# Eight split slots and four load buffers instead of six and six, weight parts made five blocks ahead within a stage, other queue orders behind the norms, and gate groups that begin with one

## The chip, the core and the metric

The kernel runs on one core of a Trainium2 chip. A core has five engines with instruction streams of their own: TensorE (PE: matmuls, with the weight load as PEld), VectorE (DVE), ScalarE (ACT), GpSimd (POOL) and SyncE (SP), which here issues the DMAs. They wait for each other by semaphores. On each engine instructions run in a fixed order, so one that waits holds up everything behind it. The metric is device time in microseconds, the median of several runs.

## The reference

Two layers work on 256 tokens of 1024 features. Layer 0 mixes by latent attention (MLA): a low-rank input projection, RMS norms, up-projections to queries, keys and values of 8 heads, rotary embedding, attention by chunks of 64, an output projection. Layer 1 mixes by sparse attention (DSA): an indexer scores keys, the best 64 keys per query are kept, then attention over those. After each mixer comes

```
x = layernorm(alpha * x + m);  f = peer(x);  x = layernorm(alpha * x + f)
```

and `peer` is a retrieval among 16384 experts:

```
q = (xt @ w_q);  s1, s2 = q against sub_keys          # 16 rows of 128 scores a token
v1, i1 = top_k(s1, 16);  v2, i2 = top_k(s2, 16)
best, pos = top_k(v1 + v2, 16);  gate = softmax(best)
a = x . w_down[expert];  y = sum(gelu(a) * gate * w_up[expert])
```

The kernel does not gather expert rows: it multiplies all tokens by all of `w_down`, places the gates of the chosen experts in a table of 256 x 16384, multiplies, and multiplies all of that by `w_up`.

## The kernel before

**Weights as a stream of blocks.** Every weight matrix is cut into blocks of 128 x 1024 f32 (512 KB), taken in one fixed order by `Stream` (`ws`). A block is loaded by SP into a buffer `raw` (pool `raws`, 6 buffers), and then split into two f16 parts: `hi` on ACT (line 89) and `lo = raw * unit - hi` on DVE (line 98). A slot of the pool `rings` (6 of them, for `hi` and for `lo`) is free again when PE has done the block. PE multiplies in three passes (hi by hi, hi by low, low by hi), which replace one f32 product. `get()` hands out the next block and has the splits emitted up to `AHEAD` = 3 blocks further (`_split`), and the loads up to `DMA_AHEAD` = 5 blocks beyond that (`_load`). A load waits until the split of the block six loads earlier has read its buffer.

**Pooled splits.** Where `ws.share` is n, every n-th block takes another way (`_pooled`): ACT scales `raw` in place (line 164) and casts it to `hi` (line 166), POOL subtracts (line 168), and ACT reads `lo` once more for a check sum (`_add`, line 177). Line 164 needs the loaded buffer but no slot of the ring.

**Stages.** In order: MLA projections and attention with `out_proj`; PEER 0: `queries` and `scores`, 128 `down` blocks in pairs, 128 `up` blocks; DSA; PEER 1 likewise. `finish` closes each stage: the last four blocks are multiplied first for token half 0, then for half 1, while half 0 goes through its `Norm` (`sums`, `square`, `centre`, `scale`, `result`); then `Turned` turns it by PE and splits it (`high` on ACT, `low` on DVE). Meanwhile PE takes the first blocks of the next stage (`open` makes `hi`, `close` makes `lo`) in units `do(t, part, k)`: token half t, one of the three products ("hh", "lh": low x by hi weights, "hl": hi x by low weights), block k. The queue helper of `finish` forces the written order on each engine.

**Choosing.** In `peer` the choice (`choose`) runs on DVE beside the first 58 `down` blocks. `spend(PACE)` is called once per block and emits as much of it as fits a written-down cost; `chains["dve"]` then holds DVE to exactly the order of emission, splits included. It ends in `gates`: four transposes on PE (`gT`, line 1177) and DVE ops that yield `gate16`, `rest` and `place16`. From then on each pair of `down` blocks has `want` groups of four tokens prepared (`prepare`: `hot` on DVE, line 1240; `gate` on POOL, line 1242, and on ACT, line 1246), and the next pair places them (`place`: matmuls `G` on PE, between the pair's matmuls and the next pair's).

**Order.** Where no chain, `issue_after` or queue helper says so, the scheduler of the language orders each engine's instructions by its own cost model, with the program's order as priority; so the order on ACT is partly decided there. In DSA, DVE is chained from the first key heads on, ACT only from the middle of `attention`.

Of the kernel before, what the change touches and what calls it, by code (L numbers as in the profile page):

```python
# [15 lines left out]
ALU = mybir.AluOpType  # L16
# [4 lines left out]
D = 1024  # L21
# [25 lines left out]
WARM = 9  # L47
EARLY = 11264
GSCALE = 2.0 ** 14
RING = 6  # L50
LAG = 4
DSA_POOL = 3
MAGIC = 12582912.0
# [1 line left out]
W_UNIT = 2.0 ** 17  # L55
# [4 lines left out]
UP_UNIT = 2.0 ** 14  # L60
# [9 lines left out]
class Split:  # L70


    def __init__(self, nc, short, cols):
        self.nc, self.short, self.cols = nc, short, cols
        self.n = {"both": 0, "most": 0}
        self.at = {"both": (0, BOTH), "most": (BOTH, BOTH + MOSTLY)}
# [24 lines left out]
class Stream:  # L101


    AHEAD = 3
    DMA_AHEAD = 5

    def __init__(self, nc, raw, rings, dtype, split, spare):
        self.nc, self.raw, self.rings, self.dtype, self.split, self.spare = nc, raw, rings, dtype, split, spare
        self.dve = self.act = lambda emit: emit()
        self.blocks, self.ready, self.kind = [], [], []  # L110
        self.n_loaded = self.n_split = self.n_taken = 0
        self.tiles = []
        self.early = {}
        self.share = 0
        self.late = {}

    def add(self, src, w=D, unit=W_UNIT, kind="both"):
        for i in range(src.shape[0]):
            self.blocks.append((src[i], w, unit))
            self.kind.append(kind)  # L120

    def parts(self, i):
        w = self.blocks[i][1]
        return [self.rings.tile([P, D], self.dtype, tag=k, name=f"{k}{i}")[:, :w] for k in ("hi", "lo")]
# [52 lines left out]
            self.act(lambda: self.nc.scalar.activation(self.spare[:, : lo.shape[1]], lo, AF.Copy, accum_out=total))  # L177

    def _split(self, upto, pooled):
        while self.n_split <= min(upto, len(self.blocks) - 1):  # L180
            i = self.n_split
            if pooled or self.share and (i - 1) % self.share == 0:
                self._pooled(i)
            else:
                self._high(i, self.act)
                self._low(i, self.dve)
            self._add(i - LAG)
            self.n_split += 1

    def get(self, ahead=None, pooled=False):  # L190
        i = self.n_taken
        self.n_taken += 1
        self.fill(i + (self.AHEAD if ahead is None else ahead), pooled)
        return self.ready[i]
# [10 lines left out]
    def close(self, i, queue):  # L205
        self._low(i, lambda emit: queue("dve", emit))
        self._load(i + self.DMA_AHEAD + 1)

    def fill(self, upto, pooled=False):
        self._split(upto, pooled)  # L210
        self._load(upto + self.DMA_AHEAD)

# [29 lines left out]
def tile_trunk(ctx: ExitStack, tc: tile.TileContext, ins, out: bass.AP, short, shared):  # L242
    nc = tc.nc
    half = F16 if short else F32R
    unit, ranks, total_unit = (UNIT, RANKS, SUM) if short else (1.0, 1.0, 1.0)
    def pool(name, bufs, **kw):
        return ctx.enter_context(tc.tile_pool(name=name, bufs=bufs, **kw))

    lead = pool("lead", 1)
    wide = pool("wide", 1)  # L250
    raws = pool("raws", 6 if short else 4)
    rings = pool("rings", RING if short else 4)
    const = pool("const", 1)
    dram = pool("dram", 1, space=bass.MemoryType.DRAM)
# [8 lines left out]
    def ps(name):  # L263
        return psp.tile([P, 512], F32, tag="ps", name=name)
# [7 lines left out]
    split = Split(nc, short, const.tile([P, BOTH + MOSTLY], F32, tag="sums", name="sums") if short else None)  # L272
# [27 lines left out]
    ws = Stream(nc, raws, rings, half, split, spare16)  # L300
    ws.add(ins["mla_h"][0:6])
    ws.add(ins["mla_qk"], unit=RANK_W_UNIT)
    ws.add(ins["mla_v"], unit=RANK_W_UNIT)
    ws.add(ins["mla_w_o"])
    ws.add(ins["peer_q"][0])
    ws.add(ins["down"][0], kind="most")
    ws.add(ins["up"][0], unit=UP_UNIT, kind="most")
    ws.add(ins["dsa_v"][0:FIRST])
    ws.add(ins["dsa_iq"])
    ws.add(ins["dsa_ik"], 576)  # L310
    ws.add(ins["dsa_v"][FIRST:NC])
    ws.add(ins["dsa_qk"])
    ws.add(ins["dsa_w_o"])
    ws.add(ins["peer_q"][1])
    ws.add(ins["down"][1], kind="most")
    ws.add(ins["up"][1], unit=UP_UNIT, kind="most")
# [90 lines left out]
    class Norm:  # L407
# [18 lines left out]
            self.queue("act", lambda: nc.scalar.activation(self.sq, self.r, AF.Square, bias=st[:, 2:3],  # L426
                                                           accum_out=st[:, 3:4]))

        def centre(self):
            st = self.st  # L430
            self.queue("dve", lambda: nc.vector.scalar_tensor_tensor(self.z, self.r, st[:, 2:3], self.g,
                                                                     op0=ALU.add, op1=ALU.mult))

        def scale(self):
            st = self.st
# [36 lines left out]
    def finish(y4, lhs_of, n, g, b, x, spare, lead=None):  # L472

        blks = [ws.get(ahead=0) for _ in range(STAGGER)]
        queue = queue_of()
        last = None
        norms = []  # L480
        for t in range(2):
            with ExitStack() as order:
                if last is not None:
                    order.enter_context(tc.issue_after(last.ins))
                for i, blk in enumerate(blks):
                    k = n - STAGGER + i
                    last = rows(y4, lhs_of(k), blk, k == 0, k == n - 1, (t,))
            if lead is not None:
                norms.append(Norm(queue, x[t], y4[t], g, b, spare[t], spare[2 + t], spare[4]))
        if lead is None:  # L490
            if short:
                judge()

            def close():
                queue = queue_of()
                for t in range(2):
                    norm = Norm(queue, x[t], y4[t], g, b, spare[t], spare[2 + t], spare[4], shared["st"][t])
                    norm.sums()
                    norm.square()
                    norm.centre()  # L500
                    norm.scale()
                    norm.result()
                for t in range(2):
                    for h, q in enumerate((nc.sync, nc.scalar)):
                        s = slice(h * 512, (h + 1) * 512)
                        q.dma_start(out[t * P : (t + 1) * P, s], spare[t][:, s])

            return close
        n0, n1 = norms
        n0.sums()  # L510
        n0.square()
        n0.centre()
        n0.scale()
        n0.result()
        nc.sync.dma_start(keep[0], spare[0])
        queue("pe", lambda: last)
        x0, x1 = Turned(queue, 0, spare[0]), Turned(queue, 1, spare[1])
        blk = [ws.open(queue) for _ in range(3)]
        n1.sums()
        x0.high(0, 2)  # L520
        x0.high(1, 4)
        n1.square()
        x0.low(0)
        n1.centre()
        blk.append(ws.open(queue))
        n1.scale()
        x0.low(1)
        n1.result()
        nc.sync.dma_start(keep[1], spare[1])
        unit = lead(queue)  # L530

        def do(t, part, *ks):
            for k in ks:
                unit(t, part, k, ws.ready[blk[k]])

        do(0, "hh", 0, 1, 2)
        do(0, "lh", 0, 1, 2)
        do(0, "hh", 3)
        do(0, "lh", 3)
        x1.high(0, 2)  # L540
        x1.high(1, 4)
        do(1, "hh", 0, 1, 2, 3)
        ws.close(blk[0], queue)
        ws.close(blk[1], queue)
        x1.low(0)
        do(0, "hl", 0, 1)
        do(1, "lh", 0, 1)
        do(1, "hl", 0, 1)
        ws.close(blk[2], queue)
        x1.low(1)  # L550
        do(0, "hl", 2)
        do(1, "hl", 2)
        do(1, "lh", 2)
        ws.close(blk[3], queue)
        do(0, "hl", 3)
        do(1, "hl", 3)
        do(1, "lh", 3)
# [491 lines left out]
    def peer(li):  # L1049
# [4 lines left out]
        s = [ar.take(16, NKEYS) for _ in range(2)]  # L1054
# [209 lines left out]
        groups = prepared = 0  # L1264
        ready = False
        for b0 in range(0, NKEYS, 2):
            p = ps(f"d{b0}")
            pv = p.rearrange("p (j t) -> p j t", t=T)
            chosen = ready
            for j in range(2):  # L1270
                proj(pv[:, j, :], ws.get())
                ready = ready or spend(PACE)
            if b0 == 0:
                chains["pe"] = None
            t0 = 4 * groups
            if t0 < T:
                nc.scalar.activation(A[:, b0 : b0 + 2, t0:], pv[:, :, t0:], AF.Gelu, scale=1.0 / unit)
            if t0 > 0:
                nc.scalar.activation(pv[:, :, :t0], pv[:, :, :t0], AF.Gelu, scale=1.0 / unit)
                nc.vector.tensor_tensor(A[:, b0 : b0 + 2, :t0], A[:, b0 : b0 + 2, :t0], pv[:, :, :t0], op=ALU.mult)  # L1280
            while groups < prepared:
                place(groups, b0 + 2)
                groups += 1
            if chosen:
                left = max(1, (NKEYS - 4 - b0) // 2)
                want = min(64 - groups, -(-(64 - groups) // left))
                assert want <= 2
                for _ in range(want):
                    prepare(prepared)
                    prepared += 1  # L1290
# [98 lines left out]

    mla()  # L1390
    peer(0)
    dsa()
    return peer(1)


# [89 lines left out]
```

## Time and profile before

| what | before |
|---|---|
| median of 3 runs | 1729.37 us (1728.97 to 1731.33) |
| profiled execution, its time | 1731.02 us |
| its span, first to last instruction | 1729.1 us |
| PE busy | 1702.9 us (98%) |
| DVE busy | 1346.9 us (78%) |
| ACT busy | 1096.5 us (63%) |
| POOL busy | 393.5 us (23%) |
| mean granted TensorE clock | 0.998 |

The span and the execution's own time differ by 1.9 us that lie outside the first and last instruction. Busy shares are means over stages with different limits, and ends of matmuls are modelled. So what counts is where PE sat idle, and which engine released it; the views named in the prediction give that.

### The profile page before, as it was taken

What the parts mean: (1) busy time and instruction counts of PE and PEld (TensorE: products, weight loads), DVE (VectorE), ACT (ScalarE), POOL (GpSimd) and SP (SyncE); (2) the same over time, 40 slices, a digit from 0 to 9 for tenths busy, and PEclk for the clock granted to TensorE, in tenths of its full rate; (3) what the DMA queues carried; (4) which work ended last, traced back from release to release, by engine and by line L of the source; (5) the groups of instructions that cost most, each with busy time, mean ns of one, the idle gap of its engine ahead of it and who ended that gap; (6) DMA issues with size and microseconds to landing.
All of it is one profiled execution on the core that took longest, in us unless ns stands there. A gap on an engine that the chain in (4) does not pass through costs nothing.

```text
span 1729.1 us, 33166 instructions
## 1 busy us (share of the span) xinstructions
PE 1702.9 (98%) x12497; PEld 1193.2 (69%) x12497; DVE 1346.9 (78%) x3033; ACT 1096.5 (63%) x1908; POOL 393.5 (23%) x257
## 2 busy tenths in 40 slices
PE   9999999999999999999998999999999999999998
PEld 7678888899984444444577698888999954444443
DVE  7679999989996566566687799999899966566565
ACT  7666556888875555555476756567888755555553
POOL 3011254555530000000022012444555400000000
PEclk9999999999999999999999999999999999999999
DMA  9445556655567666666564555566555576666662
GB/s 330 156 168 175 187 191 202 213 173 171 172 194 237 204 205 202 203 205 205 190 237 147 196 171 175 193 205 221 172 171 172 178 247 204 202 205 204 201 204 77
DMA packets 93483, 335.61 MB, mean 194 GB/s; under 512 B 10368, under 2 KB 11392, under 8 KB 93312
## 3 DMA queue, kind: packets, MB, share of 16 engines
q1 hardware_dynamic: 93024, 332.87, 59.4%
q8 instruction: 100, 1.64, 0.4%
q14 instruction: 71, 0.58, 0.1%
q10 hardware_dynamic: 288, 0.52, 0.1%
HBM read 329.16 MB, written 4.19 MB: 193 GB/s over the span
## 4 chain that ended last, share of the span: by engine, by line
PE 86%; DVE 7%; issue 3%; ACT 2%; DMA 1%; POOL 1%; DVEq 0%; SPq 0%; POOLq 0%; ACTq 0%
PE y L340 40%; PE d L340 33%; PE G L340 3%; DVE lo L98 2%; PE pq L340 2%; PE qw L340 1%; ACT hi L89 1%; PE v L340 1%; PE s L340 1%; PE o L340 1%; PE h L340 1%; DMA raw<-in_down 1%; PE ps L340 1%; PE q L340 1%; PE qi L340 1%
## 5 line engine op out<-in xcount | busy, mean ns | idle before, releaser
L98 DVE SCALAR_TENSOR_TENSOR lo<-raw,hi 128x1024 f16<-128x1024 f32 (+1 forms) x571 | 776.1, 1363 | 234.4 <-ACT hi L89 233.4
L89 ACT ACTIVATE hi<-raw 128x1024 f16<-128x1024 f32 (+1 forms) x570 | 594.8, 1051 | 294.3 <-PE y L340 183.3
L340 PE MATMUL d<-xh,lo 128*128 128x256 f16 x2048 | 558.3, 273 | 3.0 <-DVE lo L98 2.4
L340 PE MATMUL d<-xh,hi 128*128 128x256 f16 x2048 | 558.2, 273 | 0.0
L340 PE MATMUL d<-xl,hi 128*128 128x256 f16 x2048 | 558.2, 273 | 0.0
L340 PEld LDWEIGHTS <-hi 128*128 128x128 f16 x5016 | 488.5, 98 | 58.8 <-issue 1.8
L340 PEld LDWEIGHTS <-xh 128*128 128x128 f16 x2320 | 226.4, 98 | 270.6 <-ACT xh L89 2.4
L340 PE MATMUL y<-lo,xh 128*128 128x512 f16 x1088 | 326.3, 379 | 0.0
L340 PE MATMUL y<-hi,xh 128*128 128x512 f16 x1088 | 326.0, 379 | 0.0
L340 PE MATMUL y<-hi,xl 128*128 128x512 f16 x1088 | 325.6, 379 | 0.0
L340 PEld LDWEIGHTS <-lo 128*128 128x128 f16 x2508 | 245.4, 98 | 35.1 <-DVE lo L98 5.6
L1242 POOL TENSOR_TENSOR gate<-hot,gate 128x512 f16<-128x512 f16 x128 | 219.5, 1734 | 187.0 <-DVE hot L1240 187.0
L340 PEld LDWEIGHTS <-xl 128*128 128x128 f16 x1160 | 113.3, 98 | 138.2 <-DVE xl L98 2.5
L1246 ACT ACTIVATE gate<-hot,rest 128x128 f16<-128x128 f16 x512 | 165.9, 411 | 8.2 <-DVE hot L1240 8.2
L89 ACT ACTIVATE xh<-arena 128x512 f16<-128x512 f32 x131 | 82.0, 629 | 133.6 <-PE y L340 132.2
L98 DVE SCALAR_TENSOR_TENSOR xl<-arena,xh 128x512 f16<-128x512 f32 x134 | 91.9, 688 | 61.0 <-ACT xh L89 60.8
L168 POOL TENSOR_TENSOR lo<-raw,hi 128x1024 f16<-128x1024 f32 x26 | 58.1, 2234 | 192.2 <-ACT hi L166 150.8
L438 POOL TENSOR_TENSOR st<-st,mhalf 128x1 f32<-128x1 f32 x6 | 3.3, 556 | 414.2 <-DVE st L436 414.2
L164 ACT ACTIVATE raw<-raw 128x1024 f32<-128x1024 f32 x26 | 27.4, 1056 | 110.4 <-DMA raw<-in_down 91.0
L1164 POOL TENSOR_TENSOR arena<-arena 128x800 f32<-128x800 f16 x32 | 72.4, 2263 | 71.6 <-DVE arena L1161 63.4
L1240 DVE TENSOR_TENSOR hot<-iota,place 128x1024 f16<-128x1024 f16 x128 | 82.8, 689 | 6.4 <-PE G L340 3.9
L580 POOL TENSOR_SCALAR fit<-fit 128x2 f32<-128x2 f32 x1 | 0.2, 229 | 316.2 <-DVE junk L562 316.2
(210 smaller groups left out, 1578.3 us busy)
## 6 DMA issues: line engine op xcount, KB each, us to landing
raw<-in_down SPq DMA_DIRECT2D x256, 512.0 KB, 3.4
raw<-in_up SPq DMA_DIRECT2D x256, 512.0 KB, 4.2
raw<-in_peer_q SPq DMA_DIRECT2D x24, 512.0 KB, 4.6
raw<-in_dsa_qk SPq DMA_DIRECT2D x16, 512.0 KB, 4.6
raw<-in_mla_w_o SPq DMA_DIRECT2D x8, 512.0 KB, 5.3
arena<-in_peer_q SPq DMA_DIRECT2D x8, 512.0 KB, 4.9
raw<-in_dsa_v SPq DMA_DIRECT2D x8, 512.0 KB, 4.3
raw<-in_dsa_w_o SPq DMA_DIRECT2D x8, 512.0 KB, 3.8
```

What stands on the lines that cost most here:

```text
L89: return nc.scalar.copy(o, src) if unit == 1.0 else nc.scalar.mul(o, src, unit)
L98: return nc.vector.scalar_tensor_tensor(o, src, unit, hi, op0=ALU.mult, op1=ALU.subtract, accum_out=total)
L164: self.act(lambda: nc.scalar.mul(raw, raw, unit))
L168: nc.gpsimd.tensor_tensor(lo, raw, hi if short else hi.bitcast(F32), op=ALU.subtract)
L340: return pe(lambda: nc.tensor.matmul(o, l, r, start=start, stop=stop, skip_group_check=True))
L438: nc.gpsimd.tensor_tensor(st[:, 5:6], st[:, 4:5], mhalf, op=ALU.pow)
L580: nc.gpsimd.tensor_scalar(fit[:, 0:2], fit[:, 0:2], MOST * SMALL, None, op0=ALU.is_lt)
L1164: nc.gpsimd.tensor_tensor(o.rearrange("p k c -> p c k"), same, cell[t][:, h, :, None].to_broadcast([P, CELLS, TOPK]), op=ALU.mult)
L1240: nc.vector.tensor_tensor(hot, iota4[:, None].to_broadcast([P, 2, P, 4]), place16[:, :, None, four].to_broadcast([P, 2, P, 4]), op=ALU.is_ ...
L1242: nc.gpsimd.tensor_tensor(gate[:, 0], hot[:, 1].rearrange("p c j -> p j c"), gate16[:, four, None].to_broadcast([P, 4, P]), op=ALU.mult)
L1246: nc.scalar.mul(gate[:, 1, j, :], hot[:, 1, :, j], rest[:, t : t + 1])
```

## The change

The pools: `RING` becomes 8, `raws` gets 4 buffers. `AHEAD` becomes 5 and `DMA_AHEAD` 3, so `get(i)` emits the load of block i+8 as it did. `add(..., stop=True)` marks ends of stages, and `_split` does not go past the next one. In `finish` three blocks are opened, and the first closed, before the norm of half 0; the fourth is opened ahead of the norm of half 1; `x0.low(1)` goes ahead of half 1's `centre`, which is cut in two around `scale`; the order of the units on PE changes. In `peer`, `want` is 1 for the first group wherever two per pair are enough for the rest.

```diff
@@ -47,7 +47,7 @@
 WARM = 9
 EARLY = 11264
 GSCALE = 2.0 ** 14
-RING = 6
+RING = 8
 LAG = 4
 DSA_POOL = 3
 MAGIC = 12582912.0
@@ -101,10 +101,11 @@
 class Stream:
 
 
-    AHEAD = 3
-    DMA_AHEAD = 5
+    DMA_AHEAD = 3
 
     def __init__(self, nc, raw, rings, dtype, split, spare):
+        self.AHEAD = 5 if split.short else 3
+        self.stops = []
         self.nc, self.raw, self.rings, self.dtype, self.split, self.spare = nc, raw, rings, dtype, split, spare
         self.dve = self.act = lambda emit: emit()
         self.blocks, self.ready, self.kind = [], [], []
@@ -114,10 +115,12 @@
         self.share = 0
         self.late = {}
 
-    def add(self, src, w=D, unit=W_UNIT, kind="both"):
+    def add(self, src, w=D, unit=W_UNIT, kind="both", stop=False):
         for i in range(src.shape[0]):
             self.blocks.append((src[i], w, unit))
             self.kind.append(kind)
+        if stop:
+            self.stops.append(len(self.blocks))
 
     def parts(self, i):
         w = self.blocks[i][1]
@@ -177,7 +180,8 @@
             self.act(lambda: self.nc.scalar.activation(self.spare[:, : lo.shape[1]], lo, AF.Copy, accum_out=total))
 
     def _split(self, upto, pooled):
-        while self.n_split <= min(upto, len(self.blocks) - 1):
+        end = min([s for s in self.stops if s > self.n_taken], default=len(self.blocks))
+        while self.n_split <= min(upto, end - 1):
             i = self.n_split
             if pooled or self.share and (i - 1) % self.share == 0:
                 self._pooled(i)
@@ -248,7 +252,7 @@
 
     lead = pool("lead", 1)
     wide = pool("wide", 1)
-    raws = pool("raws", 6 if short else 4)
+    raws = pool("raws", 4)
     rings = pool("rings", RING if short else 4)
     const = pool("const", 1)
     dram = pool("dram", 1, space=bass.MemoryType.DRAM)
@@ -301,16 +305,16 @@
     ws.add(ins["mla_h"][0:6])
     ws.add(ins["mla_qk"], unit=RANK_W_UNIT)
     ws.add(ins["mla_v"], unit=RANK_W_UNIT)
-    ws.add(ins["mla_w_o"])
+    ws.add(ins["mla_w_o"], stop=True)
     ws.add(ins["peer_q"][0])
     ws.add(ins["down"][0], kind="most")
-    ws.add(ins["up"][0], unit=UP_UNIT, kind="most")
+    ws.add(ins["up"][0], unit=UP_UNIT, kind="most", stop=True)
     ws.add(ins["dsa_v"][0:FIRST])
     ws.add(ins["dsa_iq"])
     ws.add(ins["dsa_ik"], 576)
     ws.add(ins["dsa_v"][FIRST:NC])
     ws.add(ins["dsa_qk"])
-    ws.add(ins["dsa_w_o"])
+    ws.add(ins["dsa_w_o"], stop=True)
     ws.add(ins["peer_q"][1])
     ws.add(ins["down"][1], kind="most")
     ws.add(ins["up"][1], unit=UP_UNIT, kind="most")
@@ -426,10 +430,10 @@
             self.queue("act", lambda: nc.scalar.activation(self.sq, self.r, AF.Square, bias=st[:, 2:3],
                                                            accum_out=st[:, 3:4]))
 
-        def centre(self):
+        def centre(self, s=slice(0, D)):
             st = self.st
-            self.queue("dve", lambda: nc.vector.scalar_tensor_tensor(self.z, self.r, st[:, 2:3], self.g,
-                                                                     op0=ALU.add, op1=ALU.mult))
+            self.queue("dve", lambda: nc.vector.scalar_tensor_tensor(self.z[:, s], self.r[:, s], st[:, 2:3],
+                                                                     self.g[:, s], op0=ALU.add, op1=ALU.mult))
 
         def scale(self):
             st = self.st
@@ -507,6 +511,8 @@
 
             return close
         n0, n1 = norms
+        blk = [ws.open(queue) for _ in range(3)]
+        ws.close(blk[0], queue)
         n0.sums()
         n0.square()
         n0.centre()
@@ -515,16 +521,16 @@
         nc.sync.dma_start(keep[0], spare[0])
         queue("pe", lambda: last)
         x0, x1 = Turned(queue, 0, spare[0]), Turned(queue, 1, spare[1])
-        blk = [ws.open(queue) for _ in range(3)]
+        blk.append(ws.open(queue))
         n1.sums()
         x0.high(0, 2)
         x0.high(1, 4)
         n1.square()
         x0.low(0)
-        n1.centre()
-        blk.append(ws.open(queue))
+        x0.low(1)
+        n1.centre(slice(0, 512))
         n1.scale()
-        x0.low(1)
+        n1.centre(slice(512, D))
         n1.result()
         nc.sync.dma_start(keep[1], spare[1])
         unit = lead(queue)
@@ -533,17 +539,15 @@
             for k in ks:
                 unit(t, part, k, ws.ready[blk[k]])
 
-        do(0, "hh", 0, 1, 2)
-        do(0, "lh", 0, 1, 2)
-        do(0, "hh", 3)
-        do(0, "lh", 3)
+        do(0, "hh", 0, 1, 2, 3)
+        do(0, "lh", 0, 1, 2, 3)
+        do(0, "hl", 0)
         x1.high(0, 2)
         x1.high(1, 4)
         do(1, "hh", 0, 1, 2, 3)
-        ws.close(blk[0], queue)
         ws.close(blk[1], queue)
         x1.low(0)
-        do(0, "hl", 0, 1)
+        do(0, "hl", 1)
         do(1, "lh", 0, 1)
         do(1, "hl", 0, 1)
         ws.close(blk[2], queue)
@@ -1283,8 +1287,8 @@
                 groups += 1
             if chosen:
                 left = max(1, (NKEYS - 4 - b0) // 2)
-                want = min(64 - groups, -(-(64 - groups) // left))
-                assert want <= 2
+                assert 64 - groups <= 2 * left
+                want = min(64 - groups, 1 if 64 - groups <= 2 * (left - 1) else 2)
                 for _ in range(want):
                     prepare(prepared)
                     prepared += 1
```

## The prediction

> **What bounds the kernel now.** First the page's busy times and its chain of work that ended last, then PE's waits:
>
> ```profile
> PE 1702.9 (98%) x12497; PEld 1193.2 (69%) x12497; DVE 1346.9 (78%) x3033; ACT 1096.5 (63%) x1908; POOL 393.5 (23%) x257
> PE 86%; DVE 7%; issue 3%; ACT 2%; DMA 1%; POOL 1%; DVEq 0%; SPq 0%; POOLq 0%; ACTq 0%
> ...
> PE s L340 <- DVE arena L642: 4.6, 1, 4.6
> PE idle L1345 <- DVE iotac L293: 2.5, 1, 2.5
> PE d L340 <- DVE lo L98: 2.4, 3, 1.0
> PE G L340 <- POOL gate L1242: 1.8, 4, 0.5
> PE ps L340 <- ACT arena L372: 1.3, 1, 1.3
> PE qw L340 <- DVE xl L98: 1.3, 2, 0.8
> PE qwT L1079 <- ACT arena L372: 1.1, 1, 1.1
> PE s L340 <- ACT arena L372: 0.7, 1, 0.7
> ...
> PE d L340 <- POOL lo L168: 0.4, 1, 0.4
> ```
>
> PE bounds the kernel. No matmul is removed, so only PE's waits can be won: 4.6 + 2.4 + 1.8 + 1.3 + 1.3 + 1.1 + 0.4 = 12.9 us in places that the change touches, 0.7% of the time. A block costs PE 2.62 us, half of a pair's row in the chain, and its `hi` costs ACT 1.05 us:
>
> ```profile
> L89 ACT ACTIVATE hi<-raw 128x1024 f16<-128x1024 f32 (+1 forms) x570 | 594.8, 1051 | 294.3 <-PE y L340 183.3
> 319.00 5.24 PE d L340 x48
> ```
>
> **Deeper splits: the choosing stretches.** From the first top-16 to the last reduce of the choice (two windows, layer 0 and 1; columns: length, then PE, PEld, DVE, ACT and POOL busy), then the splits on DVE in the first, then DVE's waits in the first and the second, then where choice and `gT` transposes meet:
>
> ```profile
> 115.38:299.25 183.87, 180.38 (x1642) 160.64 (x1641) 175.10 (x554) 111.85 (x143) 62.76 (x40) 1.00 0.54 181
> 993.28:1175.66 182.38, 181.50 (x1658) 162.07 (x1656) 171.14 (x556) 111.66 (x143) 64.28 (x41) 1.00 0.57 185
> L98 DVE SCALAR_TENSOR_TENSOR lo<-raw,hi 128x1024 f16<-128x1024 f32 x54 | 79.4, 1471 | 3.5 <-ACT hi L89 3.2 <-issue 0.2
> DVE lo L98 <- ACT hi L89: 3.2, 3, 1.7
> DVE lo L98 <- ACT hi L89: 5.2, 4, 2.6
> 298.35 0.98 DVE L1168 TENSOR_REDUCE arena<-arena 128x16 f32<-128x800 f32 x1
> 299.75 0.60 PE L1177 MATMUL gT<-ident,arena 128*128 128x128 f32 x4
> 1174.76 0.97 DVE L1168 TENSOR_REDUCE arena<-arena 128x16 f32<-128x800 f32 x1
> 1175.98 0.60 PE L1177 MATMUL gT<-ident,arena 128*128 128x128 f32 x4
> ```
>
> DVE is busy 95% and 94% of these stretches, so it nearly bounds them, not PE. Two blocks more of lead are 5.2 us, more than all waits of `d` for `lo` (2.8) together. But PE must wait at `gT` for the last reduce, and it gets there only 299.75 - 299.33 = 0.4 us after it in layer 0 and 0.25 us in layer 1. The removed stall stands up again at `gT` unless DVE itself ends earlier.
>
> Counting the order of emission by the code: layer 0 has 57 splits on DVE between the first top-16 and `gates` instead of 56, layer 1 has 56 instead of 57 (the lead adds two, some go into DVE's idle time before the first top-16, and the pooled blocks shift). At the mean of 1.47 us that is +1.5 and -1.5. DVE's waits for `hi` (3.2 and 5.2) arise where ACT stands at line 164 of a pooled block whose load waits for a late split. Now each pooled block's buffer was last held by a pooled block (every fourth block, four buffers), whose split POOL makes in time; only the load ahead of it in SP's queue still hangs on DVE. I take two thirds of these waits as gone: -2.1 and -3.5. Layer 0: DVE ends 0.6 earlier, PE gains 0.6 + 0.4 = 1.0 of its 3.3 (1.6 + 0.4 + 1.3). Layer 1: DVE ends 5.0 earlier, PE gains its whole 0.9. **-1.9**; bounds -3.0 (all DVE waits gone) and +7.8 (they double: 3.2 + 1.5 - 0.4 and 5.2 - 1.5 - 0.2).
>
> **Four load buffers instead of six.** Load k hangs on split k-4 instead of k-6, and split k is emitted two blocks sooner, so a buffer has four blocks (10.5 us) between the split that frees it and the one that needs it, not six. Inside go landing (3.4), line 164 (1.06) and `hi` (1.05), 5.5 together:
>
> ```profile
> raw<-in_down SPq DMA_DIRECT2D x256, 512.0 KB, 3.4
> ACT raw L164 <- DMA raw<-in_down: 46.6, 9, 10.0
> 104.14 1.06 ACT L164 ACTIVATE raw<-raw 128x1024 f32<-128x1024 f32 x1 [3.41 <-DMA raw<-in_peer_q]
> 106.05 1.07 ACT L372 ACTIVATE arena<-qw 128x512 f32<-128x512 f32 x2
> 98.05 9.72 SPq L133 DMA_DIRECT2D raw<-in_peer_q  x5
> ```
>
> So I cost the pool at nothing of its own; the cover is 10.5 - 1.5 - 5.5 = 3.5 us, and if it goes, ACT waits with what is queued behind: PSUM copies for PE. ACT waited 46.6 us at line 164 in the first stretch already. The Trainium skill ("Perfetto Trace Analysis", Optimization Strategy) says that a gap that keeps coming back on the engine that should be full can mean that buffers are too few, which speaks against fewer of them. Here the nine waits are on ACT, and PE has 0.9 to 3.3 us of waits in a stretch, so the trace doesn't agree that they bind; by the rule the sum would grow by the third rival below.
>
> The loads behind the norm: P8's waits for the first closed block, now early; P9 to P11 wait for splits that stand behind `n1.result`, so SP issues them behind `keep[1]` and the keys, as it did five loads at 98.05. The first of those landed at 104.14, 6.1 us later, and PE has P4 to P8 to do before P9, 5 x 2.62 = 13.1 us: hidden. Behind a load that waits on SP stand the next loads and, at the start of a stage, the keys or DSA's `x`, gain and bias, which are wanted only blocks later. At 104.14 line 164 of block 33 held the copy of `qw` back, for which PE waited 1.1 us; block 33 is no longer pooled (`share` is still 0 when it is emitted), but ordinary `hi` instructions may take that place. **-0.6**, bounds -1.1 and +1.0 (one `hi` more).
>
> **DSA.** ACT, DVE and PE around 917 us:
>
> ```profile
> 913.89 1.06 ACT L164 ACTIVATE raw<-raw 128x1024 f32<-128x1024 f32 x1 [8.15 <-DMA raw<-in_dsa_w_o]
> ...
> 919.14 0.58 ACT L633 COPY arena<-q 64x512 f32<-64x512 f32 x1
> 920.41 1.27 POOL L635 TENSOR_TENSOR arena<-arena 128x512 f32<-128x512 f32 x1 [1.96 <-ACT arena L634]
> 921.71 0.69 DVE L642 TENSOR_TENSOR arena<-arena 128x512 f32<-128x512 f32 x1 [0.66 <-POOL arena L635]
> 922.46 2.93 PE s L340 x8
> ```
>
> ACT stood 8.15 us for the load of a pooled `w_o` block, with the rotary copies of the first keys behind it; PE waited 4.6. That pooled split came from `get(3, pooled=True)`. With a lead of five the same block is split by ordinary instructions in an earlier `get`, those calls emit nothing, and the one pooled block left stands in the chained part. An ordinary `hi` needs a free slot, so it isn't put so far ahead; but its load hangs on DVE, busy with the selection. I leave 1.0 us: **-3.6**, bounds -4.6 and +5.2 (ACT held two blocks longer). Three splits instead of two now stand together ahead of `keep(4)`: 1.05 us of ACT, covered by three blocks of `late`.
>
> **Norms.** PE, DVE:
>
> ```profile
> 92.96 0.60 PE L340 MATMUL qw<-hi,xl 128*128 128x512 f16 x2 [0.54 <-DVE xl L98]
> 94.26 1.04 PE L459 MATMUL xt<-ident,arena 128*128 128x128 f32 x8
> 90.95 1.28 DVE L431 SCALAR_TENSOR_TENSOR arena<-arena,st 128x1024 f32<-128x1024 f32 x1
> 92.21 0.68 DVE L98 SCALAR_TENSOR_TENSOR xl<-xt,xh 128x512 f16<-128x512 f32 x1
> 973.63 0.61 PE L340 MATMUL qw<-hi,xl 128*128 128x512 f16 x2 [0.76 <-DVE xl L98]
> 967.40 0.15 DVE L436 TENSOR_SCALAR st<-st 128x1 f32<-128x1 f32 x1 [0.57 <-ACT arena L426]
> ```
>
> `x0.low(1)` ahead of the 1.28 us `centre` ends this wait. It puts `centre` 0.7 later; the cut around `scale` wins about half of that back, since GpSimd's root now runs beside the second half (1.28 / 2 = 0.64), so `n1.result` ends some 0.3 later, an estimate. PE has one more unit of two matmuls to do meanwhile, 0.43. Net 0.55 after MLA; the same plus 0.5 after DSA, where ACT's square stood behind a line 164 that is no longer pooled; 0.2 after PEER 0. The first `close` runs where DVE has nothing else. **-1.8**, bounds -2.3 and +0.5 (0.3 later at each, uncovered, less one 0.43).
>
> **Gates.** PE, POOL:
>
> ```profile
> 311.60 0.61 PE L340 MATMUL G<-gate,hot 128*128 128x128 f16 x8 [0.33 <-POOL gate L1242]
> 308.13 3.43 POOL L1242 TENSOR_TENSOR gate<-hot,gate 128x512 f16<-128x512 f16 x2 [10.65 <-DVE hot L1240]
> ```
>
> 33 pairs stand after the choice. Before: 31 twos, then two ones; now 1, 31 twos, 1. One `gate` less (1.7 us) at the start: the first wait goes, the second mostly. **-1.6** of 1.8, bounds -1.8 and 0.
>
> **MLA.** Two splits more stand ahead during its attention (2.1 us of ACT; 2.9 of DVE at the mean of the first stretch), beside softmax work and PSUM copies that PE already waits for (0.7). I take a fifth of the two, **+1.0**, bounds 0 and +5.0.
>
> **The sum.** -1.9 - 0.6 - 3.6 - 1.8 - 1.6 + 1.0 = -8.5 us. The profiled execution took 1731.02, so 1722.5 like it; that one stands 1.65 above the median of the runs, 1729.37, which gives **1720.9**, say 1721. A measurement of this kernel can tell about 0.2%, 3.5 us, from no change.
>
> **Rivals.**
> 1. *The waits only move*: at `gT` PE waits for DVE, in DSA another `hi` waits for its load. For it: DVE's 95%, and ACT's order that a cost model decides. Against: block 33 and the `w_o` block leave their places by the code. Left are norms and gates, less MLA: -1.8 - 1.6 + 1.0 = -2.4, 1727. Chance 0.17.
> 2. *Everything goes well*: all of 12.9 and the 0.5 of ACT in the DSA norm, 1716. Against: the limit at `gT`. Chance 0.12.
> 3. *Slower: four buffers starve the choosing stretches.* DVE meets a missing `hi` at each of some ten pooled blocks per layer instead of three or four times, about 1.2 us each (3.2 over 3, 5.2 over 4): +8.4 and +7.2. All of it but 0.65 comes out at `gT`, and -8.5 + 1.9 of the other parts stand against it: +8.4, 1738. It decides once ACT holds a `hi` longer than the 3.5 us of cover. Against: the pooled chain of buffers. Chance 0.14.
>
> My forecast has 0.57, own range 1717 to 1725. Faster by over 0.2%: 0.57 + 0.12 and a little of rival 1, 0.71; within: 0.15; slower: 0.14. The range 1715.5 to 1730 leaves out the third rival and little else.
>
> **What would show it.** Right: in DSA no wait of `s` over 1.5 us; no `d` behind `lo`; `G` without POOL's wait; `qw` without `xl`; a new wait of `gT` for line 1168 of about 2 us in layer 0, none in layer 1; DVE's waits for `hi` in the stretches under 3 us a layer. Wrong: these waits above 8 us a layer (rival 3), a wait of `s` or `qwT` for ACT behind a landing load (rival 1), or new waits in MLA over 2 us.

## The result, and the profile after

| what | before | after |
|---|---|---|
| median | 1729.43 us (1726.87 to 1731.48) | 1738.07 us (1733.93 to 1746.38) |
| ratio, 95% interval | 1 | 1.0052 (1.0043 to 1.0061) |
| profiled execution, its time | 1731.02 us | 1741.35 us |
| its span | 1729.1 us | 1739.6 us |
| mean granted TensorE clock | 0.998 | 0.996 |

The change makes the kernel 0.52% slower, 8.6 us by the medians, where 8.5 us less was forecast. The profiled executions are 10.5 us apart by their spans: the one after lies 3.3 us above its median, the one before 1.6.

First the busy times on the page of the profile after the change, which hardly differ from those before:

```profile
PE 1704.3 (98%) x12497; PEld 1195.2 (69%) x12497; DVE 1349.8 (78%) x3038; ACT 1098.8 (63%) x1905; POOL 393.6 (23%) x256
```

Then its waits of PE (what waited, for what: us in total, times, the longest):

```profile
PE G L344 <- POOL gate L1246: 4.1, 4, 1.6
PE il L344 <- DVE arena L985: 3.7, 1, 3.7
PE s L344 <- DVE arena L646: 2.6, 1, 2.6
PE qw L344 <- ACT xh L89: 2.5, 2, 1.3
...
PE gT L1181 <- DVE arena L1172: 2.3, 1, 2.3
PE qn L344 <- DVE arena L642: 2.2, 1, 2.2
...
PE qwT L1083 <- ACT arena L376: 1.5, 2, 1.0
```

(Lines are 3 or 4 higher than before.) The waits of `d` for `lo`, of `ps` and of `qw` for `xl`, 2.8 + 1.3 + 1.3 us, are gone. In their place stand waits that weren't there: `il` and `qn` for rotary work on DVE (line 985 is a copy that stands behind it), `gT` for the last reduce, `qw` for `xh`, and `G` waits longer. Where the time went, by the start of the same PE instruction in both traces:

| stretch | before ends at | after ends at | lost | forecast |
|---|---|---|---|---|
| MLA, to the first turn behind it | 89.00 | 93.85 | +4.85 | +1.0 |
| norm, queries, to the first `d` | 143.93 | 148.11 | -0.67 | -1.15 |
| `down` blocks of layer 0, to the last `G` | 508.02 | 512.96 | +0.76 | -1.8 |
| `up` blocks, to the turn behind them | 844.84 | 849.77 | -0.01 | 0 |
| DSA with its opening, to the turn behind it | 969.37 | 978.67 | +4.37 | -3.8 |
| norm, queries, to the first `d` | 1021.49 | 1032.11 | +1.32 | -1.05 |
| `down` blocks of layer 1, to the last `G` | 1384.45 | 1394.71 | -0.36 | -1.7 |
| `up` blocks, to the last matmul | 1721.19 | 1731.45 | 0.00 | 0 |

MLA and DSA hold 9.2 of the 10.3 us.

**MLA.** ACT of both kernels around the rotary copies of `krope` (start, duration; in brackets the idle time before and what ended it), before, then after with PE's next matmul:

```profile
24.61 1.06 ACT L89 ACTIVATE hi<-raw 128x1024 f16<-128x1024 f32 x1 [0.80 <-PE krope L340]
25.69 0.36 ACT L633 COPY arena<-krope 32x256 f32<-32x256 f32 x1
```

```profile
22.27 1.06 ACT L89 ACTIVATE hi<-raw 128x1024 f16<-128x1024 f32 x1 [0.80 <-DMA raw<-in_mla_qk]
...
25.99 1.06 ACT L89 ACTIVATE hi<-raw 128x1024 f16<-128x1024 f32 x1 [0.48 <-DMA raw<-in_mla_qk]
28.38 1.06 ACT L89 ACTIVATE hi<-raw 128x1024 f16<-128x1024 f32 x1 [1.33 <-DMA raw<-in_mla_qk]
29.46 0.36 ACT L637 COPY arena<-krope 32x256 f32<-32x256 f32 x1
...
31.49 0.27 PE L344 MATMUL qn<-V,hi 128*128 128x256 f16 x1 [2.22 <-DVE arena L642]
```

Before, the `hi` ahead of the copies waited for PE. After, four `hi` from 22.27 to 28.38 wait for loads (0.80, 0.58, 0.48 and 1.33 us), and the copies come 3.8 us later; PE's next `qn` waits for the rotary work on DVE behind them (line 642) and stands 2.2 us.

**DSA.** ACT, DVE and PE of the kernel after, at the indexer:

```profile
872.93 1.06 ACT L89 ACTIVATE hi<-raw 128x1024 f16<-128x1024 f32 x1 [2.29 <-DMA raw<-in_dsa_v]
874.01 0.58 ACT L637 COPY arena<-qi 32x512 f32<-32x512 f32 x1
...
887.63 0.41 DVE L978 TENSOR_TENSOR arena<-arena 64x256 f32<-64x256 f32 x1
...
888.19 3.06 PE L344 MATMUL il<-arena 64*128 64x128 f32 x16 [3.72 <-DVE arena L985]
```

The same: the copies of `qi` stand behind a `hi` whose load landed late; before, the first of them was at 864.81, and line 974, which is line 978 now, at 875.57. Of these differences 4.9 us come from the stages ahead of DSA. Before, `il` began at 879.01 without a wait, and took 1.71 us, not 3.06. The lead may have a part in it too: from the first copy of `qi` to that of `ki` ACT has five `hi` to make instead of three, and needs 9.75 us instead of 8.1.

The wait of `s` has the same cause, at a `w_o` block that is now split by the ordinary two instructions:

```profile
927.35 1.06 ACT L89 ACTIVATE hi<-raw 128x1024 f16<-128x1024 f32 x1 [3.60 <-DMA raw<-in_dsa_w_o]
```

The rotary copies (line 637) come at 928.43, and `s` begins at 931.75.

**The clock behind a wait.** Windows of the kernel after: behind the wait in MLA, behind the wait of `il`, and behind that of `s` (length, then busy us of PE, PEld, DVE, ACT, POOL; then the granted clock, the share of the DMA engines, GB/s):

```profile
32.60:36.00 3.40, 3.40 (x19) 2.47 (x17) 3.00 (x6) 3.11 (x5) 0.73 (x1) 0.51 0.73 228
888.20:892.40 4.20, 4.20 (x19) 3.19 (x20) 1.75 (x2) 1.86 (x4) 2.12 (x1) 0.50 0.72 230
...
931.70:935.20 3.50, 3.45 (x27) 3.06 (x28) 3.50 (x5) 1.49 (x2) 1.97 (x1) 1.00 0.37 110
```

From 1.1 us behind the wait of 2.2 us PE ran 3.4 us at half clock, and behind that of 3.7 us another 4.2: 1.7 + 2.1 us more. These two waits are thus paid 1.8 and 1.6 times. Behind the 2.6 us of `s` the clock stayed whole.

**The end of the choice.** DVE and POOL of the kernel after in layer 0, from the last reduce to the first gate:

```profile
302.68 0.97 DVE L1172 TENSOR_REDUCE arena<-arena 128x16 f32<-128x800 f32 x1
...
308.35 1.22 DVE L98 SCALAR_TENSOR_TENSOR lo<-raw,hi 128x1024 f16<-128x1024 f32 x1 [1.26 <-ACT hi L89]
...
313.29 0.69 DVE L1244 TENSOR_TENSOR hot<-iota,place 128x1024 f16<-128x1024 f16 x1
314.06 1.96 POOL L1246 TENSOR_TENSOR gate<-hot,gate 128x512 f16<-128x512 f16 x1 [12.26 <-DVE hot L1244]
```

From the end of the last reduce, 303.65, to `hot` DVE needs 9.6 us; before it was 8.0 (299.33 to 307.36), with five splits between in both. One of these now waits 1.26 us for its `hi`, which waits for its load. So `G` waits longer for the single gate than it did for two.

### The profile page after: what moved, and what is told of

It reads as the page before. It is cut to its first block, busy times and chain, and to the rows that moved or that the text cites. A ratio compares the mean times of both kernels' runs of the same rounds, so it can differ in the third digit from the quotient of the medians.

```text
span 1739.6 us, 33260 instructions
## 1 busy us (share of the span) xinstructions
PE 1704.3 (98%) x12497; PEld 1195.2 (69%) x12497; DVE 1349.8 (78%) x3038; ACT 1098.8 (63%) x1905; POOL 393.6 (23%) x256
## 4 chain that ended last, share of the span: by engine, by line
PE 76%; DVE 13%; issue 4%; DMA 3%; ACT 3%; POOL 1%; DVEq 0%; SPq 0%; POOLq 0%; ACTq 0%
PE y L344 39%; PE d L344 27%; DVE lo L98 5%; PE G L344 3%; PE pq L344 3%; ACT hi L89 1%; DVE arena L1172 1%; DMA raw<-in_peer_q 1%; DMA raw<-in_down 1%; DVE arena L1113 1%; DVE arena L1110 1%; PE ps L344 1%; DVE arena L1165 1%; PE q L344 1%; PE s L344 1%
## 5 line engine op out<-in xcount | busy, mean ns | idle before, releaser
L89 ACT ACTIVATE hi<-raw 128x1024 f16<-128x1024 f32 x571 | 598.4, 1051 | 342.1 <-PE y L344 181.8
L344 PE MATMUL G<-gate,hot 128*128 128x128 f16 x1024 | 68.3, 219 | 4.1 <-POOL gate L1246 4.1
```

The costliest lines, as they stand in the source:

```text
L89: return nc.scalar.copy(o, src) if unit == 1.0 else nc.scalar.mul(o, src, unit)
L344: return pe(lambda: nc.tensor.matmul(o, l, r, start=start, stop=stop, skip_group_check=True))
```

## The experiments

### The parts alone: which of them costs

> The kernel before with the slots alone: eight ring slots, four load buffers, parts five blocks ahead, the stops; the old order behind the norms and the old gates. Theory A (this part alone makes the change slower, since ACT then stands at splits whose load has not landed and the copies for TensorE stand behind it, in MLA and DSA): about +9 us, 1738, with the wait of qn for DVE of about 2 us in MLA and the wait of il for DVE of about 3.7 us in DSA. Theory B (the new orders behind the norms cost, the slots gain as predicted): about -4 us, 1725, and neither of the two waits.

The edit: of the change only the hunks on `RING`, `Stream`, `raws` and `stop`. Measured **1738.59 us, ratio 1.0057 (1.0041 to 1.0073)**. Theory A holds: by the medians this part alone is as slow as the whole change. Its waits:

```profile
PE G L344 <- POOL gate L1246: 3.9, 5, 1.4
PE qw L344 <- ACT xh L89: 3.3, 2, 1.7
PE il L344 <- DVE arena L978: 2.6, 1, 2.6
...
PE qn L344 <- DVE arena L642: 1.9, 1, 1.9
```

The waits of `qn` and `il` are there, and also those of `G` and of `qw` for `xh`, though gates and orders are the old ones.

> The kernel before with the new orders behind the norms alone. Theory A: within 1.5 us of the time before, since a third early split finds no free slot with six of them and the waits of qw that are left are those that the early splits in front of xh cause (under 1.5 us in all); 1728 to 1730. Theory B: at least +4 us, 1733 or more, with waits of qw for ACT's xh of 2 us in all or more.

The edit: only the hunks in `Norm.centre` and `finish`. Measured **1731.74 us, ratio 1.0010 (1.0001 to 1.0019)**: a little slower, where the forecast had 1.8 us less. That is 0.6 us over theory A's bound and far from theory B's 4 us. Its waits:

```profile
PE qw L340 <- ACT xh L89: 1.2, 1, 1.2
PE xt L459 <- DVE arena L443: 1.0, 3, 0.5
```

The 1.3 us of `qw` for `xl` became 1.2 for `xh` and 1.0 of `xt` for the later `n1.result`. By the traces 1.1 us are lost behind PEER 0, from the turn to the first `qi` (8.0 us instead of 6.9).

> The kernel before with the new spacing of the gates alone (1, then 31 twos, then 1). As predicted: -1.6 us, 1727.8, with the wait of G for POOL under 0.5 us (1.8 before). Rival (the longer waits of G after the change come from the spacing itself, since the first product follows sooner behind the choice): +1.5 to +2.5 us, 1731 to 1732, with a wait of G for POOL of about 4 us.

```diff
-                want = min(64 - groups, -(-(64 - groups) // left))
+                want = min(64 - groups, 1 if 64 - groups <= 2 * (left - 1) else 2)
```

Measured **1726.92 us, ratio 0.9983 (0.9975 to 0.9992)**. As forecast: no wait of `G` is left among PE's waits, and from the first to the last `G` the two layers gain 1.0 us each. The trace gains more ahead of the first `G`, where `d` waits 1.0 us for `lo` instead of 2.4; the edit doesn't touch that place.

> The kernel before with four load buffers instead of six and nothing else (six slots, parts three blocks ahead). If the buffers alone are the cause (A1): +4 to +9 us, 1733 to 1738, with the waits of qn for DVE in MLA and of il for DVE in DSA as after the change, and loads that land later than the split that wants them. If it is the lead of five with four buffers together, or the lead alone (A2): within 1.5 us of the time before, 1728 to 1731, because a buffer then still has four blocks and the splits come two blocks later.

```diff
-    raws = pool("raws", 6 if short else 4)
+    raws = pool("raws", 4)
```

Measured **1737.68 us, ratio 1.0042 (1.0029 to 1.0055)**. Two buffers fewer, and nothing else, cost 8.1 us by the medians, as theory A1 had it; slots and lead on top of that (1738.59) make no difference that can be told. By the stretches of the table above this trace loses 7.1 us in MLA, and 1.2 in DSA although `s` doesn't wait there any more. `qn` waits 2.7 us, and `il` 4.4 in two. Windows of MLA's start and of DSA's projections, in the order before, four buffers, after the change:

```profile
6.00:20.00 14.00, 12.77 (x109) 10.39 (x108) 12.39 (x31) 10.16 (x16) 1.88 (x2) 1.00 1.01 394
864.00:870.00 6.00, 6.00 (x57) 5.56 (x56) 3.89 (x8) 5.73 (x8) 1.28 (x1) 1.00 1.02 411
```

```profile
6.00:20.00 14.00, 13.52 (x115) 11.26 (x114) 12.82 (x31) 9.63 (x15) 1.53 (x2) 1.00 0.89 326
864.00:870.00 6.00, 6.00 (x57) 5.38 (x56) 3.00 (x7) 2.52 (x4) 0.00 (x0) 1.00 0.82 250
```

```profile
6.00:20.00 14.00, 11.87 (x105) 9.92 (x104) 12.08 (x29) 9.35 (x14) 1.04 (x1) 1.00 0.87 306
864.00:870.00 6.00, 6.00 (x57) 5.39 (x56) 4.17 (x8) 3.11 (x4) 0.00 (x0) 1.00 0.84 266
```

Before, the DMA engines are busy through these windows (shares 1.01 and 1.02): there is next to no room to make up for a load that starts late. With four buffers a load waits for the split of the block four loads earlier, the shares fall to 0.89 and 0.82, and 394 GB/s become 326. The `hi` of the block behind `krope` waits 1.65 us for its load, and PE 2.7:

```profile
27.75 1.06 ACT L89 ACTIVATE hi<-raw 128x1024 f16<-128x1024 f32 x1 [1.65 <-DMA raw<-in_mla_qk]
28.83 0.36 ACT L633 COPY arena<-krope 32x256 f32<-32x256 f32 x1
...
31.03 0.27 PE L340 MATMUL qn<-V,hi 128*128 128x256 f16 x1 [2.73 <-ACT arena L372]
```

### One buffer given back

> The changed kernel with five load buffers instead of four (the room comes from a scratch tile of one reduction and from spare copies of small tiles), all else as changed. Theory A1 (the loads that come too late for lack of buffers cost most): each load starts a block sooner, so at least half of the 8 us that four buffers cost alone comes back, with the waits of qn for DVE in MLA (2.2) and of il for DVE in DSA (3.7) together under 3 us; 1732 to 1735 us. Rival A2 (with parts five blocks ahead the splits themselves stand in front of the copies, whether their loads are there or not): 1737 to 1739 and both waits as before.

```diff
-    raws = pool("raws", 4)
+    raws = pool("raws", 5 if short else 4)
-        square = small.tile([P, BOTH], F32, tag="square", name="square", bufs=1)
+        square = rest[:, :BOTH]
```

(and `bufs=2` for the tiles `gm` and `gs`, 8 columns for `ones`.) Measured **1734.54 us, ratio 1.0029 (1.0019 to 1.0038)**, within the time of theory A1, though the 3.5 us that come back by the medians are a little less than the half that it named. The wait of `il` is gone, and `qn` waits 0.3 us. MLA moves 362 GB/s, against 306 of the changed kernel. MLA's window again, then PE's longest waits:

```profile
6.00:20.00 14.00, 13.48 (x115) 11.25 (x114) 12.91 (x31) 10.69 (x17) 2.46 (x2) 1.00 0.96 362
```

```profile
PE gT L1181 <- DVE arena L1172: 3.8, 2, 2.9
PE ps L344 <- ACT arena L376: 2.7, 2, 2.2
PE qw L344 <- ACT xh L89: 2.5, 2, 1.3
```

What is left over the time before lies at these places. By the stretches of the table MLA loses only 0.9 us in this trace and DSA gains 2.7, but the queries of layer 1 lose 2.1 and its `down` blocks 3.0. Behind the waits of 2.9 us (`gT`) and 2.2 us (`ps`) PE runs at half clock again (0.52 for 3.4 us, 0.50 for 3.2). The `ps` wait still stands behind a load: line 167 waited 4.35 us for a `down` block. Six buffers with eight slots weren't run; already the fifth needed room from other tiles.

### The lead

> The changed kernel with parts three blocks ahead and loads five behind them, as before the change; eight slots, four buffers, orders and gates as changed. If the lead of five is what takes the w_o block of DSA away from GpSimd: the wait of s for DVE of about 4.6 us is there again and the time is 1740 to 1744. If four buffers alone shift that wait (as they did with six slots, where s waited under 0.5 us): 1736 to 1739. In both cases the waits of qw for xh stay above 2 us, since the slots and not the lead let the four splits in.

```diff
-    DMA_AHEAD = 3
+    DMA_AHEAD = 5
-        self.AHEAD = 5 if split.short else 3
+        self.AHEAD = 3
```

Measured **1742.44 us, ratio 1.0095 (1.0080 to 1.0111)**: with eight slots and four buffers the lead of five is worth some 4 us by the medians, so it isn't what hurts. The time falls within the first expectation, but not for its reason: `s` has no wait for DVE. The `w_o` block is GpSimd's again, yet ACT waited only 1.4 us for its load, and behind the copies, which began at 925.67:

```profile
928.26 1.06 ACT L167 ACTIVATE raw<-raw 128x1024 f32<-128x1024 f32 x1 [1.41 <-DMA raw<-in_dsa_w_o]
```

The waits of `qw` for `xh` are there (3.3 us in two), as eight slots let them.

### Behind the norms

> The changed kernel with the lead kept back behind each norm: one block ahead at the first block taken after a norm, then one more with each block up to five. Four load buffers as changed. Theory C (the eight slots let four splits of later blocks go in front of x0's upper parts on ScalarE, 3.9 us of it, and TensorE waits for those): the wait of qw for ACT's xh goes from 2.5 to under 0.8 us, the time by 1.5 to 2 us, to 1736 to 1737. Rival: the splits that are put off stand in front of the copies of qw a few us later, so qwT or ps waits longer by the same and the time stays within 1 us of 1738.

```diff
         self.n_taken += 1
         self.fill(i + (self.AHEAD if ahead is None else ahead), pooled)
+        self.AHEAD = min(self.AHEAD + 1, 5 if self.split.short else 3)
...
         ws.close(blk[3], queue)
+        ws.AHEAD = 1
```

Measured **1743.52 us, ratio 1.0077 (1.0063 to 1.0090)**: both expectations missed. It didn't do what it was for. The four splits stand in front of `xh` as before, though the program now emits them later; so it is the scheduler that puts them there, as it does before the change with the two for which there are slots:

```profile
92.25 3.88 ACT L89 ACTIVATE hi<-arena 128x1024 f16<-128x1024 f32 x4
96.04 1.11 ACT L89 ACTIVATE xh<-xt 128x256 f16<-128x256 f32 x3
```

Elsewhere a wait is new (3.4 us of `o` for ACT in DSA, behind a `hi` that waits 2.4 us for a `w_o` load); that it comes from the fewer blocks made early isn't shown.

> The changed kernel with five load buffers and the lead kept back behind each norm, both as in the two experiments of these. If A1 and C both hold and their gains add up: 1730 to 1733 us. If only C holds: 1736 to 1737. If neither: 1737 to 1739.

Measured **1732.92 us, ratio 1.0024 (1.0014 to 1.0035)**. The time is within the first expectation, but not for its reason: `qw` waits 2.5 us for `xh` here too, so C doesn't hold. The kernel can't be told from that with five buffers alone (1.0029); the gain is that of the buffer.

> The changed kernel with the splits of the blocks behind a norm's first four held back on ScalarE until x1's square is issued; slots, buffers, lead and order as changed. (A lead that grows from one did not do this: the four splits still stood in front of x0's upper parts.) Theory C: the wait of qw for ACT's xh goes from 2.5 to under 0.8 us and the norm after MLA and the one after DSA each end about 1 us sooner; 1735 to 1737 us. Rival: four splits in a row then stand in front of x1's upper parts and the copies of qw, qw or qwT waits for those, and the time stays within 1 us of 1738.

```diff
+    def hold(behind):
+        emit_act, left = ws.act, [NC]
+        def held(emit):
+            left[0] -= 1
+            if left[0] == 0:
+                ws.act = emit_act
+            with tc.issue_after(behind.ins):
+                return emit_act(emit)
+        ws.act = held
...
         ws.close(blk[3], queue)
+        hold(n1.at)
```

(`n1.at` is the instruction of x1's square on ACT.)

Measured **1737.13 us, ratio 1.0045 (1.0031 to 1.0058)**. PE's waits:

```profile
PE o L344 <- ACT arena L712: 3.3, 2, 2.8
...
PE qw L344 <- ACT xh L89: 0.8, 2, 0.4
```

The mechanism is shown: with the splits behind them, `xh` is waited for 0.8 us, not 2.5. The time can't be told from the changed kernel's (1.0052), and theory and rival meet at it. From the turn to the first `qw` PE needs 1.2 us less behind MLA and behind DSA, but to the first `d` only 0.6 and 0.3 of it are left, and `qwT` waits 1.9 us instead of 1.5, as the rival had it. In DSA `o` now waits 2.8 us for ACT (1.4 before this edit), a place that the edit doesn't touch; why is open.

> The kernel with the new gates and the unpooled w_o block, and of the new order behind the norms only this: x0's second lower part goes ahead of x1's centring. If the forecast's step holds (qw's waits for xl of 1.3 us go, the later x1 costs 0.3 at each of three norms): -0.4 to -1.3 us, 1717 to 1718. Rival, as the new order alone went (1731.7 against 1729.6): +1 to +2 us, with waits of xt for DVE in the place of those for xl.

```diff
         x0.low(0)
+        x0.low(1)
         n1.centre()
...
         n1.scale()
-        x0.low(1)
```

Measured **1720.13 us, ratio 0.9947 (0.9934 to 0.9961)**, against 0.9934 (0.9921 to 0.9946) of the kernel below without this edit: no gain, and by the medians the loss of 1.8 us that the rival named, though the intervals overlap. Of `qw` for `xl` nothing is left, and `xt` waits 1.6 us for `n1.result` in three places instead.

### The `w_o` block that GpSimd split

> The kernel before with the new spacing of the gates, and with the w_o block of DSA that GpSimd split made by the ordinary two instructions (six slots, six buffers, lead of three). The forecast's DSA term: the wait of s for DVE goes from 4.6 to at most 1.5, so about 3.6 us less than with the gates alone, 1723 to 1724. Rival: the upper part's instruction waits on ScalarE for the same load in the same place, the wait of s stays above 2.5 us, and the time is 1725.5 to 1727.

```diff
-            return heads(kT, h, ahead=(3, 2), pooled=True)
+            return heads(kT, h, ahead=(3, 2))
```

Measured **1718.37 us, ratio 0.9934 (0.9921 to 0.9946)**: 11 us under the kernel before and 8.5 under the gates alone, more than twice the 3.6 of the forecast. PE and its window, first of the kernel with the gates alone, then the same matmuls of this kernel:

```profile
919.35 2.62 PE L340 MATMUL s<-arena 128*128 128x128 f32 x8 [4.97 <-DVE arena L642]
```

```profile
919.30:923.00 3.70, 3.65 (x14) 2.77 (x15) 3.70 (x12) 2.98 (x6) 2.48 (x2) 0.56 0.41 130
```

```profile
914.15 1.48 PE L340 MATMUL s<-arena 128*128 128x128 f32 x8
```

```profile
914.10:917.80 3.70, 3.70 (x32) 3.26 (x31) 2.79 (x10) 3.49 (x4) 1.22 (x1) 1.00 0.56 187
```

The wait of 5.0 us is gone, and with it the half clock behind it, 1.8 us up to the first `o`. By the stretches of the table DSA takes 7.1 us less than with the gates alone. Of the expectation's rival nothing is seen: the ordinary `hi` waits for PE, not for its load.

> As the experiment with x0's second lower part first, and the turn of pooled splits in PEER set two blocks later, so that block 33 is split by the ordinary two instructions. If the forecast's step for block 33 holds: 0.6 us less (0 to 1.1) than that kernel, by the wait of qwT for ACT of 1.1 us; 1716.5 to 1717.5. Rival: an ordinary upper part waits there for the same load: no gain, and up to 1 us more.

```diff
         queries(4)
-        ws.share = POOLED
         scores(0)
         queries(6)
+        ws.share = POOLED
```

Measured **1717.06 us, ratio 0.9938 (0.9924 to 0.9952)**. PE's waits of `qwT` (0.8 us) and `ps` (1.3 to 0.2) for ACT go, so the step for block 33 holds; from the norm behind MLA to the first `d` PE needs 2.7 us less, far more than the 0.6 that it was priced at. By the interval the kernel can't be told from the one before it without both edits (0.9934). These two, six slots, six buffers and a lead of three, beat both the kernel before and the change.

## Why the prediction was wrong

**The step that failed** is "so I cost the pool at nothing of its own". Its cover of 3.5 us was worked out for blocks of 2.62 us and a landing of 3.4 us, both of the `down` stretches, where the DMA share is 0.54. MLA and DSA were never held against it; in the windows shown of them the share is 1.0. There loads that started late left ACT standing at a `hi` (1.65 us in MLA with four buffers, 3.60 in DSA after the change), with copies for PE queued behind. Two buffers fewer cost 8.1 us alone, and that is the sign of the result. The third rival had the cause (buffers) and, by luck, the time (1738), but the wrong place: in the choosing stretches DVE waited for `hi` under 3 us a layer, as the forecast had said. The first rival's two waits came (`gT` for DVE, `s` behind another `hi`), and so did two signs of being wrong, the wait of `s` behind a landing load and a new wait in MLA over 2 us (`qn`, 2.2).

- **Too few buffers.** The Trainium skill ("Perfetto Trace Analysis", Optimization Strategy) takes a recurring gap as a sign of too few buffers, and the forecast answered that the trace doesn't agree. With four buffers alone PE does wait for want of them, but in single places (2.7 us of `qn`, 4.4 of `il`), not in a gap that repeats: the rule's cause is borne out, its sign isn't.
- **MLA, +1.0** (bounds 0 to +5.0): mis-sized, +4.85. It counted the splits that move ahead, not the loads.
- **DSA, -3.6**: the wait of `s` for the pooled block was the right one to go for, and its price was too low: 7.4 us between the spans of the runs with and without it (1724.6 and 1717.2), since the clock behind the wait wasn't counted. In the change it came to +4.4: `s` still waited 2.6 us for a `hi` behind a load, 3.7 of `il` were new, with half clock behind them. The lead of five does take the block from GpSimd, which has it again with a lead of three; but the lead isn't needed for the wait to go: with four buffers and a lead of three it went too.
- **Norms, -1.8**: wrong alone (+2.1 by the medians) and in the change. The wait for `xl` went, as said. But two waits took its place: `xh` behind up to four splits of later blocks, which eight slots let in, and the one for the later `n1.result` (1.0 us alone). The forecast counted slots for the stretch and not for the norm, where a free slot is filled at once.
- **Gates, -1.6**: right alone (-2.7 by the medians, -2.0 in the `G` stretches). In the change it was lost to DVE's backlog behind the choice.
- **Choosing, -1.9**: half right. No `d` waits for `lo`; `gT` waits 2.3 us in layer 0 and next to nothing in layer 1, as said; layer 0 got one split more and layer 1 one fewer. But the forecast let the backlog end at `gT`. It goes on to `hot`, and with the gates the two layers came to +0.4 instead of -3.5. All kernels with a lead of five waited 4.2 us or more at `gT` and `G` together, none with a lead of three more than 2.4.
- **Block 33, -0.6**: nothing in the change, where an ordinary `hi` took the place and waits for its load too (the bound of +1.0 named it; row below); right in its mechanism with six buffers, where it was worth more (2.7).

```profile
110.64 1.06 ACT L89 ACTIVATE hi<-raw 128x1024 f16<-128x1024 f32 x1 [5.19 <-DMA raw<-in_peer_q]
111.60 1.06 ACT L376 ACTIVATE arena<-qw 128x512 f32<-128x512 f32 x2
```

What stays open is what eight slots and a lead of five would bring with six buffers, and how much of the 5 us that are left with five buffers is the missing sixth: by the trace of that run nearly all of the loss in MLA and DSA is back, and what is left stands at the queries, `gT` and the `down` blocks.

## What to carry to other kernels

A buffer count is checked against each stage that shares the pool, by its DMA share and its time per block, and above all where the DMA engines have no slack; a cover worked out in the longest stage says nothing of the shortest. Room that is freed ahead of an urgent instruction gets filled, by a scheduler that goes by its own costs: what must not stand there has to be ordered, not just emitted later. And a wait on PE of some us is to be priced with the half clock that can follow it.

## What the runs showed of the hardware that was not expected

**Half clock behind short waits.** A spell of about 3.4 us at a granted clock of 0.50 to 0.56 followed waits of 5.0 us (`s`, gates alone), 2.9 and 2.2 (`gT` and `ps`, five buffers), 2.7 (`qn`, four buffers) and 2.2 (`qn`, after), but neither the 2.6 of `s` after the change nor the 2.8 of `o` with the splits held:

```profile
31.80:35.20 3.40, 3.40 (x19) 2.40 (x17) 2.54 (x5) 2.27 (x4) 0.73 (x1) 0.50 0.69 216
```

```profile
958.50:961.30 2.80, 0.12 (x1) 0.00 (x0) 1.68 (x6) 2.44 (x5) 0.00 (x0) 1.00 0.90 291
961.40:965.00 3.60, 3.60 (x19) 2.31 (x20) 2.01 (x6) 3.51 (x6) 0.00 (x0) 1.00 0.73 258
```

(four buffers alone, then the splits held.) So not every wait of this size is paid twice. The executions of the changed kernel spread over 12 us, and the clock goes with it: those with a mean granted clock of 0.998 took 1735.1 us on average, those with 0.994 1744.2. The Trainium skill ("TensorE: Matmul & The Clock Gate", Part 1: The HAM clock gate) has the half rate follow at least one idle window of about 3.4 us, with windows that run freely; the length of the spells agrees, but waits well under a window were enough here, and freely running windows would be one reason why one wait is followed and another isn't; no run here shows that reason.

**Load buffers and the rate of the loads.** From 6 to 20 us, in MLA, the loads of 512 KB moved at 394 GB/s with six buffers and 326 with four (six slots and a lead of three in both), and at 362 with five and 306 with four (eight slots and a lead of five). How many transfers were under way at a time was not measured. At `krope` the kernel before showed no sign of it: there the `hi` ahead of the copies waited for PE.
